# Planes of h's second block in the triple buffers, an earlier combine, and four seven-product pairs in feed-forward groups 5 and 9

## Chip, cores and metric

The kernel runs on one core of one Trainium2 chip. The metric is the device time of one execution in microseconds. The time before is 2090.94 us, the median of three runs (2088.95 to 2092.37).

## What is computed

A trunk of two pre-norm residual layers on x of 1 x 256 x 2048 in float32, and a final RMS norm. Layer 0 mixes with sliding-window attention beside an mLSTM, layer 1 with forgetting attention (FoX). The change lies in what follows each mixer: the output projection and the SwiGLU feed-forward network (FFN, hidden width 5632).

```python
for layer in range(2):
    xn = rms_norm(h, norm_mix[layer])
    mix = swa_mlstm(xn) @ w_out_even  if layer == 0 else  fox(xn) @ w_out_odd
    h = h + mix
    xn = rms_norm(h, norm_ffn[layer])
    h = h + (silu(xn @ w_gate[layer]) * (xn @ w_up[layer])) @ w_down[layer]
return rms_norm(h, norm_final)
```

## The kernel before

**Precision.** Each float32 operand is split into two fp32r parts, hi = cast(x) and lo = x - hi; a product takes three matmuls, hi·xh, lo·xh and hi·xl, of 128 x 128 weights of the moving side against 512 columns. Weights stream from memory: `load_raw` (L145) issues a DMA of 512 KB (two k-tiles by 512 columns) on SyncE's queue (SP), ScalarE (ACT) casts hi (L206), VectorE (DVE) subtracts to get lo (L207), and TensorE (PE) reads both. A split chunk lives in one of five slots of the stock.

**FFN groups.** The 5632 hidden columns are 11 groups of 512, in parts of 3, 4 and 4 (groups 0 to 2, 3 to 6, 7 to 10); behind each part stand two down-projection groups of the same build. `pair_group` works one group as eight pairs of k-tiles, each pair against two weight matrices (gate and up). A *plain* pair takes two chunks and 24 matmuls. A *seven-product* pair (kind 1, a Strassen-like scheme) takes 21 matmuls: both chunks are loaded into one raw buffer of the list `quads` (`quad`, 128 x 2048), three quarters of it are cast and subtracted as one 128 x 1536 operation into a triple buffer (L380 on ACT, L381 on DVE; the triples are `hi0`, `lo0` and `hi1`, `lo1`, used in turn), then DVE forms differences in place in the raw buffer (L645 on 128 x 1024, L648 and L649 on 128 x 512), and two 128 x 1024 casts and subtractions (L380, L381 again) fill two slots. Its seven products go into the group's four accumulators `plain` and into four further ones, `prods`. Sums of x that the scheme needs are made once per layer (`sx`, and `x4` for pair 7).

`ORDER` sets the pairs of a group: seven-product pairs stand at places 1, 3 and 5 of 0 to 7. `HEAVY` has them at places 0, 2, 4 and 6; a group in `DENSE` uses it, and `DENSE` is empty. `combine` (L575 to L592) merges `prods` into a tile c: ACT copies prods[0] (L577), DVE adds prods[3] (L579), prods[2] (L580) and prods[1] (L581). In a gate/up or down group (`halves` is None) it is called behind the loop over the pairs. DVE then adds the four `plain` accumulators to c (L696), and silu and the product with up follow (L698, L700). The eight banks of the accumulators change roles from group to group: the banks of `prods` hold `plain` of the next group and the other way round.

**Output projection and start of the FFN.** `out_proj` makes h in four blocks n = 0 to 3 of 512 columns. For each, `split_turned` copies the 16-bit planes of the block into a scratch `box` (L338, ACT), turns them with four DMA transposes of 128 x 4 x 128 (L340, SP's queue), and a `join` put off by `LATER` steps puts the planes together again (L345, ACT) and splits them into xh and xl (ACT L386, DVE L387). `scrap` (L365 to L376) gives the box: n = 0 and 2 use c, n = 3 uses `sd0` and `sd1`, which nothing else needs by then, and n = 1 a buffer with the tag `quad`, one of the two that `quads` gets later. A third raw buffer, `own`, is taken from a place of the weight pool (`wp`, tag `hi`); `quads` is in turn Q0, own, Q1.

**What sets the order.** Code order sets priorities; the framework's scheduler then orders each engine's instructions by its own estimate of when each can run, and PE, DVE, ACT and SP each work through their list in order. Buffers force waits: a load into a `quad` buffer that served as a box comes behind the join that reads it.

Of the kernel before, what the change touches and what calls it, by code (L numbers as in the profile page):

```python
# [7 lines left out]
F32 = mybir.dt.float32  # L8
BF16 = mybir.dt.bfloat16
F32R = mybir.dt.float32r  # L10
# [7 lines left out]
P = 128  # L18
# [5 lines left out]
NB = 512  # L24
CK = 2
# [10 lines left out]
ORDER = ((0, 0), (1, 1), (0, 2), (1, 3), (0, 4), (1, 5), (0, 6), (0, 7))  # L36
HEAVY = ((1, 1), (0, 0), (1, 3), (0, 2), (1, 5), (0, 4), (1, 7), (0, 6))
FOURTH = 7
DENSE = ()
DOWN = {  # L40
    6: ((0, 0), (1, 1), (0, 2), (1, 3), (0, 4), (0, 5)),
    8: ((0, 0), (1, 1), (0, 2), (1, 3), (0, 4), (1, 5), (0, 6), (0, 7)),
# [12 lines left out]
QUADS = 2  # L55
# [13 lines left out]
def mixed_of(order):  # L69
    return [p for w, p in order if w]  # L70
# [5 lines left out]
def trunk(  # L76
# [27 lines left out]
    stock, triples, quads = [], [], []  # L104
# [94 lines left out]
    def load_chunk(w, k0, c0, n):  # L199
        raw = ahead.pop(0) if ahead else load_raw(w, k0, c0, n)  # L200
        return raw if isinstance(raw, tuple) else split_chunk(raw, n)
# [10 lines left out]
    def two_banks(par, name):  # L212
        return [(pm if par else pa).tile([P, NB], F32, tag="pm" if par else "acc", name=name) for _ in range(2)]
# [153 lines left out]
    def scrap(fp, n):  # L367
        if n % 2 == 0:
            box = fp.tile([P, 4, NB], F32, tag="c", name="box", bufs=1)
            halves = box[:, 0:2, :], box[:, 2:4, :]  # L370
        elif n == 3:
            halves = [fp.tile([P, 3, NB], F32, tag=f"sd{i}", name="box", bufs=1)[:, 0:CK, :] for i in range(2)]
        else:
            box = fp.tile([P, 2 * CK, NB], F32, tag="quad", name="box", bufs=QUADS)
            halves = box[:, 0:2, :], box[:, 2:4, :]
        flat, turned = (a.rearrange("p a n -> p (a n)") for a in halves)  # L376
        return flat, turned.bitcast(U16).rearrange("p (b k t q) -> p b k t q", b=2, t=NT, q=P)

# [177 lines left out]
    def three(o, ah, al, hi, lo, start, stop):  # L556
        nc.tensor.matmul(o, ah, hi, start=start, stop=False)  # L557
        nc.tensor.matmul(o, ah, lo, start=False, stop=False)  # L558
        nc.tensor.matmul(o, al, hi, start=False, stop=stop)  # L559

    def pair_group(fp, par, lhs, sums, mats, order, todo=(), halves=None, inner=None, raws=None):
# [3 lines left out]
        def fresh(*at):  # L565
            known = at in begun
            begun.add(at)
            return not known

        todo = list(todo)  # L570
        prods = None
        kinds = [kind for kind, _ in order]
# [20 lines left out]

        for pos, (kind, pair) in enumerate(order):
            k0 = 2 * pair
            if inner is not None and pos == len(order) - 1:
                c = combine(prods)
                inner()
            if not kind:
# [4 lines left out]
                for m, (w, c0) in enumerate(mats):  # L604
                    hi, lo = load_chunk(w, k0, c0, NB)
# [10 lines left out]
            if first:  # L616
                if 1 - par and halves:
                    prods = [pm.tile([P, NB], F32, tag="pm", name="prod") for _ in range(4)]
                else:
                    prods = two_banks(1 - par, "prod") + two_banks(1 - par, "prod")  # L620
# [40 lines left out]
            three(prods[2], sh[2], sl[2], *parts[3], first, last)  # L661
            three(prods[3], sh[1], sl[1], *parts[2], first, last)
            three(plain[0][1], xa[:, t1], la[:, t1], *parts[0], fresh(0, 1), False)
        if inner is None:
            c = combine(prods)
        return plain, c

    def ffn(layer, fp, sx, x4, sd, key, todo, idx_next=None, key_next=None, finish=None):
# [8 lines left out]
        for g0, g1 in zip(PARTS, PARTS[1:]):  # L677
# [3 lines left out]
            for g in range(g0, g1):  # L681
                par = (g1 - 1 - g) % 2
                plain, c = pair_group(
                    fp,
                    par,
                    x_of,
                    sums_x,
                    [(w_gate[layer], g * NB), (w_up[layer], g * NB)],
                    HEAVY if g in DENSE else ORDER,
                    todo,  # L690
# [105 lines left out]
    def close_layer(layer, w_out, idx, key, **rest):  # L796
        with tc.tile_pool(name=f"fp{layer}", bufs=2) as fp:
            junk_of[:] = fp, "tmp", 2
            nx = len(mixed_of(ORDER))
            nd = max(len(mixed_of(o)) for o in DOWN.values())  # L800
            sx = [fp.tile([P, nx, 4, P], F32R, name=f"sx{i}", bufs=1) for i in range(2)]
            x4 = fp.tile([P, 2, P], F32R, name="x4", bufs=1)
            todo = out_proj(w_out, idx, key, (*sx, x4, fp))
            sd = [fp.tile([P, nd, 4, P], F32R, tag=f"sd{i}", name=f"sd{i}", bufs=1) for i in range(2)]
            triples.extend([fp.tile([P, 3, NB], F32R, name=f"{a}{i}", bufs=1) for a in ("hi", "lo")] for i in range(2))
            stock.extend([slot() for _ in range(5)])
            own = wp.tile([P, 2, CK, NB], F32R, tag="hi", name="raw").rearrange("p a k n -> p (a k) n").bitcast(F32)
            quads.extend(fp.tile([P, 2 * CK, NB], F32, tag="quad", name="raw", bufs=QUADS) for _ in range(QUADS))
            quads.insert(1, own)
            ffn(layer, fp, sx, x4, sd, key, todo, **rest)  # L810
            stock.clear()
            triples.clear()
            quads.clear()
# [3 lines left out]
    hi, lo = slot()  # L817
# [17 lines left out]
    with tc.tile_pool(name="ev", bufs=1) as ev:  # L835
# [225 lines left out]
        with tc.tile_pool(name="mp", bufs=1) as mp:  # L1061
# [8 lines left out]
            halves = spare_halves()  # L1070
# [11 lines left out]
            c = pair_even(OFF_QM, OFF_KM, MIXQ, [(G3_AT, gates_3)])  # L1082
# [30 lines left out]
            c = pair_even(OFF_OM, OFF_VM, MIXV, todo)  # L1113
# [80 lines left out]
    with tc.tile_pool(name="od", bufs=1) as od:  # L1194
# [70 lines left out]
        halves = spare_halves()  # L1265
# [9 lines left out]
        for i in range(4):  # L1275
            qt = od.tile([P, 4, S], F32, tag="qt", name="qtf")
            kt = od.tile([P, 4, S], F32, tag="kt", name="ktf")
            c = pair_nat(i * NB, FOX_H * FD + i * NB, todo if i == 0 else [(P_JOIN, join_p)] if join_p else (), MIX if i else MIX0, rest)
# [12 lines left out]
            if i == 0:  # L1291
                todo, later[:] = list(later), []
                c = pair_nat(c_v, c_v + NB, todo)
# [124 lines left out]
```

## Time and profile before

| | |
|---|---|
| time before, median of 3 runs | 2090.94 us (2088.95 to 2092.37) |
| time of the profiled execution | 2090.14 us |
| its span, first to last instruction | 2088.4 us |
| granted TensorE clock, mean | 0.998 |
| busy: PE / DVE / ACT | 2071.4 / 1806.3 / 1367.1 us |
| read from memory | 408.68 MB, 197 GB/s |

Times within the span are counted in microseconds from its first instruction. "Idle before" is the engine's wait ahead of an instruction, and the name behind the arrow is what ended it. In a table by stretches, each engine has its busy time and in brackets the number of instructions; "PEclk" is the clock that was granted to TensorE. The busy time of a matmul of 128 x 512 shows as 389 ns although they start some 0.226 us apart (184 in 41.50 us), since they overlap.

### The profile page before, as it was taken

The numbers are of one execution on the slowest core, as the hardware profiler recorded it, in microseconds if no ns is written. First come the engines' busy times: TensorE is split into PE (matmuls) and PEld (weight loads), VectorE is DVE, ScalarE is ACT, GpSimd is POOL, SyncE is SP. The second block draws the span as 40 slices with busy tenths as digits, with TensorE's granted clock in tenths as the row PEclk, the third lists the DMA queues.
The fourth block names the chain that finished last, engine by engine and source line by source line (L and its number), as shares of the span: only waits on it lengthen the run. The fifth ranks groups of instructions, "written<-read, shape, count | busy, mean of one in ns | idle before, by whom it ended". The sixth has DMA issues, their size and how long they took to land.

```text
span 2088.4 us, 26470 instructions
## 1 busy us (share of the span) xinstructions
PE 2071.4 (99%) x9473; PEld 1714.7 (82%) x9473; DVE 1806.3 (86%) x2169; ACT 1367.1 (65%) x1649; POOL 44.0 (2%) x69
## 2 busy tenths in 40 slices
PE   9999999999999999999999999999999999999998
PEld 7878887888888888888888888877888888888887
DVE  6788768989999989998899688679989999999984
ACT  6777677665577646667677676587655667556763
POOL 1010000000000000000000001000000000000000
PEclk9999999999999999999999999999999999999999
DMA  8566577765677666665676776585756766666754
GB/s 292 174 207 194 188 242 215 222 200 198 205 221 224 210 194 224 217 209 184 203 202 218 225 200 185 155 269 188 250 188 196 233 196 217 226 205 200 235 158 159
DMA packets 309572, 434.84 MB, mean 208 GB/s; under 512 B 106413, under 2 KB 114625, under 8 KB 309313
## 3 DMA queue, kind: packets, MB, share of 16 engines
q1 hardware_dynamic: 307088, 426.27, 65.1%
q0 software_dynamic: 1632, 5.80, 0.9%
q8 instruction: 74, 1.21, 0.2%
q10 hardware_dynamic: 720, 1.09, 0.2%
q14 instruction: 58, 0.47, 0.1%
HBM read 408.68 MB, written 2.12 MB: 197 GB/s over the span
## 4 chain that ended last, share of the span: by engine, by line
PE 89%; ACT 4%; DVE 3%; DMA 2%; issue 2%; SPq 0%; POOL 0%; POOLq 0%; ACTq 0%; DVEq 0%
PE acc L558 20%; PE acc L559 20%; PE acc L557 20%; PE prod L558 5%; PE prod L557 5%; PE prod L559 5%; PE acc L245 4%; PE acc L244 4%; PE acc L246 4%; DVE hi L207 1%; ACT box L345 1%; PE p L411 1%; ACT hi L206 1%; ACT hi L380 1%; DMA raw<-in_w_gate_dram 1%
## 5 line engine op out<-in xcount | busy, mean ns | idle before, releaser
L206 ACT CAST hi<-raw 128x1024 fp32r<-128x1024 f32 (+3 forms) x561 | 567.1, 1023 | 366.5 <-PE acc L559 179.4
L207 DVE TENSOR_TENSOR hi<-raw,hi 128x1024 fp32r<-128x1024 f32 (+3 forms) x561 | 657.9, 1186 | 137.2 <-ACT hi L206 134.7
L559 PE MATMUL acc<-hi,xl 128*128 128x512 f32 x1320 | 511.9, 389 | 0.0
L557 PE MATMUL acc<-hi,xh 128*128 128x512 f32 x1320 | 495.9, 390 | 0.8 <-ACT xh L386 0.6
L380 ACT CAST hi<-raw 128x1024 fp32r<-128x1024 f32 (+2 forms) x299 | 344.9, 1168 | 225.8 <-PE acc L559 192.7
L558 PE MATMUL acc<-hi,xh 128*128 128x512 f32 x1254 | 488.0, 390 | 0.2 <-DVE hi L207 0.2
L557 PEld LDWEIGHTS acc<-hi,xh 128*128 128x128 f32 x1320 | 247.6, 188 | 53.5 <-ACT xh L386 1.8
L559 PEld LDWEIGHTS acc<-hi,xl 128*128 128x128 f32 x1320 | 248.0, 188 | 51.5
L558 PEld LDWEIGHTS acc<-hi,xh 128*128 128x128 f32 x1254 | 235.4, 188 | 50.0 <-DVE hi L207 1.0
L381 DVE TENSOR_TENSOR hi<-raw,hi 128x1024 fp32r<-128x1024 f32 (+1 forms) x204 | 240.2, 1180 | 11.1 <-ACT hi L380 10.4
L381 DVE TENSOR_TENSOR lo<-raw,hi 128x1536 fp32r<-128x1536 f32 x95 | 166.6, 1754 | 43.6 <-ACT hi L380 40.0
L559 PE MATMUL acc<-hi,ml 128*128 128x512 f32 x466 | 181.0, 389 | 0.0
L557 PE MATMUL acc<-hi,mh 128*128 128x512 f32 x466 | 173.3, 389 | 0.0
L558 PE MATMUL acc<-hi,mh 128*128 128x512 f32 x437 | 170.3, 390 | 0.4 <-DVE hi L207 0.4
L245 PE MATMUL acc<-hi,mh 128*128 128x512 f32 (+1 forms) x322 | 126.3, 392 | 0.0
L244 PE MATMUL acc<-hi,mh 128*128 128x512 f32 (+1 forms) x322 | 125.8, 391 | 0.0
L246 PE MATMUL acc<-hi,ml 128*128 128x512 f32 (+1 forms) x322 | 123.7, 391 | 0.0
L645 DVE TENSOR_TENSOR raw<-raw 128x1024 f32<-128x1024 f32 x95 | 115.5, 1217 | 0.4
L557 PEld LDWEIGHTS acc<-hi,mh 128*128 128x128 f32 x466 | 87.5, 188 | 18.6 <-ACT hi L206 0.4
L559 PEld LDWEIGHTS acc<-hi,ml 128*128 128x128 f32 x466 | 87.5, 188 | 18.1
L245 PE MATMUL acc<-hi,xh 128*128 128x512 f32 (+3 forms) x288 | 99.8, 347 | 0.2 <-DVE hi L207 0.2
L246 PE MATMUL acc<-hi,xl 128*128 128x512 f32 (+3 forms) x288 | 99.1, 345 | 0.0
(364 smaller groups left out, 3073.9 us busy)
## 6 DMA issues: line engine op xcount, KB each, us to landing
raw<-in_w_gate_dram SPq DMA_DIRECT2D x176, 512.0 KB, 4.3
raw<-in_w_up_dram SPq DMA_DIRECT2D x176, 512.0 KB, 4.8
raw<-in_w_down_dram SPq DMA_DIRECT2D x176, 512.0 KB, 4.8
raw<-in_w_in_odd_dram SPq DMA_DIRECT2D x88, 512.0 KB, 5.2
raw<-in_w_in_even_dram SPq DMA_DIRECT2D x51, 512.0 KB, 5.0
raw<-in_w_out_even_dram SPq DMA_DIRECT2D x32, 512.0 KB, 5.3
raw<-in_w_out_odd_dram SPq DMA_DIRECT2D x32, 512.0 KB, 4.7
hr<-in_w_in_even_dram SPq DMA_DIRECT2D x12, 512.0 KB, 4.4
```

The costliest lines, as they stand in the source:

```text
L206: latest[0] = nc.scalar.copy(hi[:, k, 0:n], raw[:, k, 0:n])
L207: nc.vector.tensor_tensor(out=lo[:, k, 0:n], in0=raw[:, k, 0:n], in1=hi[:, k, 0:n].bitcast(F32), op=ALU.subtract)
L244: nc.tensor.matmul(o, ah[:, ts], hi, start=(k == 0), stop=False)
L245: nc.tensor.matmul(o, ah[:, ts], lo, start=False, stop=False)
L246: nc.tensor.matmul(o, al[:, ts], hi, start=False, stop=(k == k_all - 1 and cs.stop == n))
L345: nc.scalar.copy(ju[:, :, b], turned[:, b, :, :, :].rearrange("p k t q -> p (k t q)"))
L380: cast = nc.scalar.copy(dst_h, src)
L381: nc.vector.tensor_tensor(out=dst_l, in0=src, in1=dst_h.bitcast(F32), op=ALU.subtract)
L557: nc.tensor.matmul(o, ah, hi, start=start, stop=False)
L558: nc.tensor.matmul(o, ah, lo, start=False, stop=False)
L559: nc.tensor.matmul(o, al, hi, start=False, stop=stop)
L645: nc.vector.tensor_tensor(out=raw[:, 1:4:2, :], in0=raw[:, 3:4, :].broadcast_to([P, 2, NB]), in1=raw[:, 1:3, :], op=ALU.subtract)
```

## The change

Four edits. `DENSE` becomes (5, 9), so that groups 5 and 9 of both layers take pair 7 as a fourth seven-product pair. The box of h's second block (n = 1) is taken from the second triple (`hi1` for the planes, `lo1` for the turned ones) and no longer from a `quad` buffer; the triples get tags for that. `combine` of a gate/up or down group is called right behind the last seven-product pair: ahead of place 6 of `ORDER`, of place 7 of `HEAVY`, of place 4 of the six-pair down groups. And `own` becomes the third of the raw buffers: Q0, Q1, own.

```diff
--- before.py
+++ after.py
@@ -36,7 +36,7 @@
 ORDER = ((0, 0), (1, 1), (0, 2), (1, 3), (0, 4), (1, 5), (0, 6), (0, 7))
 HEAVY = ((1, 1), (0, 0), (1, 3), (0, 2), (1, 5), (0, 4), (1, 7), (0, 6))
 FOURTH = 7
-DENSE = ()
+DENSE = (5, 9)
 DOWN = {
     6: ((0, 0), (1, 1), (0, 2), (1, 3), (0, 4), (0, 5)),
     8: ((0, 0), (1, 1), (0, 2), (1, 3), (0, 4), (1, 5), (0, 6), (0, 7)),
@@ -371,8 +371,7 @@
         elif n == 3:
             halves = [fp.tile([P, 3, NB], F32, tag=f"sd{i}", name="box", bufs=1)[:, 0:CK, :] for i in range(2)]
         else:
-            box = fp.tile([P, 2 * CK, NB], F32, tag="quad", name="box", bufs=QUADS)
-            halves = box[:, 0:2, :], box[:, 2:4, :]
+            halves = [fp.tile([P, 3, NB], F32, tag=f"{a}1", name="box", bufs=1)[:, 0:CK, :] for a in ("hi", "lo")]
         flat, turned = (a.rearrange("p a n -> p (a n)") for a in halves)
         return flat, turned.bitcast(U16).rearrange("p (b k t q) -> p b k t q", b=2, t=NT, q=P)
 
@@ -593,6 +592,8 @@
 
         for pos, (kind, pair) in enumerate(order):
             k0 = 2 * pair
+            if 1 not in kinds[pos:] and 1 in kinds[pos - 1 : pos] and halves is None:
+                c = combine(prods)
             if inner is not None and pos == len(order) - 1:
                 c = combine(prods)
                 inner()
@@ -661,7 +662,7 @@
             three(prods[2], sh[2], sl[2], *parts[3], first, last)
             three(prods[3], sh[1], sl[1], *parts[2], first, last)
             three(plain[0][1], xa[:, t1], la[:, t1], *parts[0], fresh(0, 1), False)
-        if inner is None:
+        if inner is None and halves is not None:
             c = combine(prods)
         return plain, c
 
@@ -802,11 +803,11 @@
             x4 = fp.tile([P, 2, P], F32R, name="x4", bufs=1)
             todo = out_proj(w_out, idx, key, (*sx, x4, fp))
             sd = [fp.tile([P, nd, 4, P], F32R, tag=f"sd{i}", name=f"sd{i}", bufs=1) for i in range(2)]
-            triples.extend([fp.tile([P, 3, NB], F32R, name=f"{a}{i}", bufs=1) for a in ("hi", "lo")] for i in range(2))
+            triples.extend([fp.tile([P, 3, NB], F32R, tag=f"{a}{i}", name=f"{a}{i}", bufs=1) for a in ("hi", "lo")] for i in range(2))
             stock.extend([slot() for _ in range(5)])
             own = wp.tile([P, 2, CK, NB], F32R, tag="hi", name="raw").rearrange("p a k n -> p (a k) n").bitcast(F32)
             quads.extend(fp.tile([P, 2 * CK, NB], F32, tag="quad", name="raw", bufs=QUADS) for _ in range(QUADS))
-            quads.insert(1, own)
+            quads.append(own)
             ffn(layer, fp, sx, x4, sd, key, todo, **rest)
             stock.clear()
             triples.clear()
```

Counted over the program, PE has 12 matmuls of 128 x 512 fewer (three for each of four groups); DVE has 16 instructions more and ACT four, those of four seven-product pairs in place of plain ones; SP's count of 973 stays. Lines behind L592 stand one further, and L377 to L592 one less: L380 and L381 of before are L379 and L380 after, L577 is L576.

Three places show how the order moves. The first is SP's queue in layer 0, at the end of the output projection's first half; the eight transposes are four for each block. `box_2579` and `box_2647` are the boxes of n = 0 and 1, `raw_2993` of before is Q0, `raw_2994` and `raw_2995` of after are Q0 and Q1. Before:

```order
L145 DMA raw_2764<-in_w_out_even_dram 128x2x512
L145 DMA raw_2781<-in_w_out_even_dram 128x2x512
L340 DMA_TRANSPOSE box_2579<-box_2579 128x4x128 x4
L340 DMA_TRANSPOSE box_2647<-box_2647 128x4x128 x4
L145 DMA raw_2798<-in_w_out_even_dram 128x2x512
L145 DMA raw_2815<-in_w_out_even_dram 128x2x512
L145 DMA raw_2832<-in_w_out_even_dram 128x2x512
L145 DMA raw_2869<-in_w_out_even_dram 128x2x512
L145 DMA raw_2993<-in_w_gate_dram 128x2x512
L145 DMA raw_2993<-in_w_up_dram 128x2x512
L145 DMA raw_2886<-in_w_out_even_dram 128x2x512
```

After:

```order
L145 DMA raw_2697<-in_w_out_even_dram 128x2x512
L145 DMA raw_2994<-in_w_gate_dram 128x2x512
L145 DMA raw_2714<-in_w_out_even_dram 128x2x512
L145 DMA raw_2994<-in_w_up_dram 128x2x512
L145 DMA raw_2731<-in_w_out_even_dram 128x2x512
L145 DMA raw_2995<-in_w_gate_dram 128x2x512
L145 DMA raw_2995<-in_w_up_dram 128x2x512
L145 DMA raw_2748<-in_w_out_even_dram 128x2x512
L145 DMA raw_2765<-in_w_out_even_dram 128x2x512
L340 DMA_TRANSPOSE box_2579<-box_2579 128x4x128 x4
L340 DMA_TRANSPOSE box_2648<-box_2647 128x4x128 x4
L145 DMA raw_2782<-in_w_out_even_dram 128x2x512
```

Both loads of the first two seven-product pairs (four DMAs) now stand ahead of the eight transposes, and one more load of w_out stands behind them.

The second is ACT some 30 us later, where the joins of n = 2 (`box_2922`, after: `box_2923`) and of n = 3 (`box_2969`/`box_2970`, after: `box_2970`/`box_2971`) stand among the casts for group 0. Before, where `raw_2992` is `own`, of the second seven-product pair, and `raw_2994` is Q1, of the third:

```order
L206 CAST hi_2987<-raw_3088 128x1024
L380 CAST hi0_2983<-raw_2994 128x1536
L345 COPY box_2969<-box_2970 128x1024 x2
L206 CAST hi_2990<-raw_3156 128x1024
L380 CAST hi1_2985<-raw_2992 128x1536
L345 COPY box_2922<-box_2922 128x1024 x2
L386 ACTIVATE xh_58<-box_2969,gT_93 128x256 x4
L206 CAST hi_2991<-raw_3172 128x1024
L386 ACTIVATE xh_58<-box_2922,gT_93 128x256 x4
```

After, where `raw_2995` is Q1, of the second pair, and `raw_2993` is `own`, of the third:

```order
L206 CAST hi_2988<-raw_3089 128x1024
L345 COPY box_2923<-box_2923 128x1024 x2
L379 CAST hi_2989<-raw_2995 128x1024
L385 ACTIVATE xh_58<-box_2923,gT_93 128x256 x4
L326 ACTIVATE full_3119<-box_2923,gT_93 128x256 x2
L379 CAST hi_2990<-raw_2995 128x1024
L206 CAST hi_2991<-raw_3157 128x1024
L379 CAST hi0_2984<-raw_2993 128x1536
L345 COPY box_2970<-box_2971 128x1024 x2
L206 CAST hi_2992<-raw_3173 128x1024
L379 CAST sx0_2332<-s4_3122 128x512
L385 ACTIVATE xh_58<-box_2970,gT_93 128x256 x4
```

The 128 x 1536 cast of the second pair has gone from this place (it stands 15 rows further up, a few rows behind the join of n = 1, whose box it overwrites), the join of n = 2 has come ahead of that of n = 3, and the second pair's 128 x 1024 casts stand ahead of the latter.

The third is DVE at the beginning of group 5 in layer 0, right behind the drain of group 4's last accumulator into c. Before:

```order
L696 TENSOR_TENSOR c_4905<-acc_4633,c_4905 128x512
L207 TENSOR_TENSOR hi_2991<-raw_5014,hi_2991 128x1024
L700 SCALAR_TENSOR_TENSOR c_4905<-c_4905,r_2998 128x512
L381 TENSOR_TENSOR lo1_2986<-raw_2993,hi1_2985 128x1536
L700 SCALAR_TENSOR_TENSOR c_4905<-c_4905,r_2998 128x512
L381 TENSOR_TENSOR hi_2987<-raw_2994,hi_2987 128x1024
L645 TENSOR_TENSOR raw_2993<-raw_2993 128x2x512
L648 TENSOR_TENSOR raw_2993<-raw_2993 128x512
L381 TENSOR_TENSOR hi_2988<-raw_2994,hi_2988 128x1024
L649 TENSOR_TENSOR raw_2993<-raw_2993 128x512
L207 TENSOR_TENSOR hi_2989<-raw_5062,hi_2989 128x1024
L207 TENSOR_TENSOR hi_2990<-raw_5078,hi_2990 128x1024
```

After:

```order
L697 TENSOR_TENSOR c_4831<-acc_4634,c_4831 128x512
L380 TENSOR_TENSOR lo1_2987<-raw_2994,hi1_2986 128x1536
L701 SCALAR_TENSOR_TENSOR c_4831<-c_4831,r_2999 128x512
L207 TENSOR_TENSOR hi_2989<-raw_5047,hi_2989 128x1024
L646 TENSOR_TENSOR raw_2994<-raw_2994 128x2x512
L701 SCALAR_TENSOR_TENSOR c_4831<-c_4831,r_2999 128x512
L380 TENSOR_TENSOR lo0_2985<-raw_2995,hi0_2984 128x1536
L649 TENSOR_TENSOR raw_2994<-raw_2994 128x512
L380 TENSOR_TENSOR hi_2992<-raw_2993,hi_2992 128x1024
L380 TENSOR_TENSOR hi_2990<-raw_2994,hi_2990 128x1024
L646 TENSOR_TENSOR raw_2995<-raw_2995 128x2x512
L207 TENSOR_TENSOR hi_2988<-raw_5031,hi_2988 128x1024
```

Before, one subtraction of 128 x 1536 and two plain chunks (L207) stand here behind the drain, besides a third ahead of it; after, two of the former and two of the latter, so the raw work of two seven-product pairs (L646, L649) has moved close together.

## The prediction

> **What bounds the kernel now.** I read the page first, for the engine that sets the end.
>
> ```profile
> span 2088.4 us, 26470 instructions
> ...
> PE 2071.4 (99%) x9473; PEld 1714.7 (82%) x9473; DVE 1806.3 (86%) x2169; ACT 1367.1 (65%) x1649; POOL 44.0 (2%) x69
> ...
> L558 PE MATMUL acc<-hi,xh 128*128 128x512 f32 x1254 | 488.0, 390 | 0.2 <-DVE hi L207 0.2
> ```
>
> PE is busy 99% of the span, and over 1254 matmuls with a lo operand it waited 0.2 us for DVE. So only two things are worth anything: fewer matmuls, and the few places where PE stands still. DVE at 86% is close behind, so work that is given to it needs cover. I then read the stretches around the start of the FFN in layer 0 (330 to 362 us) and layer 1 (1400 to 1424), beside the present groups 5 (602.0) and 9 (850.9).
>
> ```profile
> 330.00:340.00 10.00, 9.14 (x41) 7.24 (x39) 6.14 (x8) 6.01 (x6) 0.69 (x1) 1.00 0.82 220
> 340.00:350.00 10.00, 7.36 (x23) 4.86 (x24) 9.82 (x17) 10.00 (x16) 0.00 (x0) 0.83 0.54 178
> 350.00:362.00 12.00, 11.01 (x49) 8.69 (x48) 12.00 (x14) 9.20 (x12) 0.00 (x0) 1.00 0.51 177
> ```
>
> ```profile
> 1400.00:1412.00 12.00, 10.52 (x44) 7.46 (x43) 11.41 (x19) 12.00 (x19) 0.00 (x0) 1.00 0.53 176
> 1412.00:1424.00 12.00, 11.47 (x47) 8.21 (x46) 12.00 (x16) 9.85 (x12) 0.00 (x0) 1.00 0.53 177
> ```
>
> ```profile
> 602.00:643.50 41.50, 41.50 (x184) 34.36 (x184) 40.43 (x45) 28.51 (x28) 0.00 (x0) 1.00 0.73 226
> 850.90:892.40 41.50, 41.50 (x184) 34.36 (x183) 39.25 (x44) 28.16 (x28) 0.00 (x0) 1.00 0.68 216
> ```
>
> In a steady group PE is busy all the time: 41.50 us / 184 = **0.2255 us per matmul**. At that rate the 32 us from 330 would hold 142 matmuls; 41 + 23 + 49 = 113 ran, 29 short: **6.5 us lost** in layer 0. In layer 1, 24 us hold 106.4, 91 ran: 15.4 short, **3.5 us lost**. The single waits come from PE's rows in time.
>
> ```profile
> 341.17 0.50 PE L557 MATMUL prod<-hi,xh 128*128 128x512 f32 x1 [2.03 <-ACT hi L380]
> ...
> 342.96 0.80 PE L558 MATMUL prod<-lo,xh 128*128 128x512 f32 x1 [0.83 <-DVE lo L381]
> 343.56 0.63 PE L559 MATMUL prod<-hi,xl 128*128 128x512 f32 x1
> 343.98 0.63 PE L558 MATMUL acc<-lo,xh 128*128 128x512 f32 x1
> ...
> 346.53 0.50 PE L557 MATMUL acc<-hi,xh 128*128 128x512 f32 x1 [0.64 <-ACT xh L386]
> ...
> 355.40 0.50 PE L558 MATMUL prod<-hi,sx 128*128 128x512 f32 x1 [0.99 <-DVE hi L381]
> ```
>
> The first two waits are for the cast and the subtraction of the second seven-product pair, the third for xh of h's third block (n = 2), the fourth for a late slot. Together 4.5 us; behind them matmuls start 0.42 us apart for a while, at a granted clock of 0.83 in that stretch. The Trainium skill ("TensorE: Matmul & The Clock Gate", Part 1) says that the clock halves after an idle window of about 3.4 us and returns after a busy one. The trace agrees in kind (0.42 us against 0.2255), though here gaps of 2.03 and 0.83 us were enough; by that rule the slow matmuls vanish with the gaps, which the count of 29 already contains.
>
> Why the pair is late stands in the rows of SP's queue and of ACT.
>
> ```profile
> 280.48 10.37 SPq L340 DMA_TRANSPOSE box<-box  x8
> 290.94 2.06 SPq L145 DMA_DIRECT2D raw<-in_w_out_even_dram  x4
> ...
> 323.47 5.61 SPq L340 DMA_TRANSPOSE box<-box  x4
> 329.18 0.53 SPq L145 DMA_DIRECT2D raw<-in_w_gate_dram  x1
> 329.80 5.14 SPq L340 DMA_TRANSPOSE box<-box  x4
> 335.00 0.58 SPq L145 DMA_DIRECT2D raw<-in_w_up_dram  x1
> ```
>
> ```profile
> 336.28 2.56 ACT L345 COPY box<-box 128x1024 uint16<-128x1024 uint16 x2 [3.99 <-DMA box<-box]
> 338.70 1.04 ACT L206 CAST hi<-raw 128x1024 fp32r<-128x1024 f32 x1
> 339.64 1.47 ACT L380 CAST hi<-raw 128x1536 fp32r<-128x1536 f32 x1
> 341.01 2.55 ACT L345 COPY box<-box 128x1024 uint16<-128x1024 uint16 x2
> 343.43 1.70 ACT L386 ACTIVATE xh<-box,gT 128x256 fp32r<-128x256 f32 x4
> ```
>
> The pair's raw buffer is `own`; its up load is issued at 335.00, behind the four transposes of n = 3, and its cast runs at 339.64, just ahead of the wait that ends at 341.17. ACT meanwhile takes the join of n = 3 first (idle 3.99 us for it) and that of n = 2 only at 341.01, though the latter's transposes were issued six us earlier. In layer 1 ACT shows the same:
>
> ```profile
> 1397.71 1.48 ACT L380 CAST hi<-raw 128x1536 fp32r<-128x1536 f32 x1 [2.31 <-DMA raw<-in_w_up_dram]
> 1399.10 5.01 ACT L345 COPY box<-box 128x1024 uint16<-128x1024 uint16 x4
> ```
>
> **The change, part by part.** *Box and `own`.* The order of the changed kernel issues the loads of the first two pairs ahead of the first transposes, some 55 us before 335.00, casts the second pair behind the join of n = 1 instead of at 339.64, and joins n = 2 ahead of n = 3. `own` is now the third pair, whose loads still stand behind both blocks of transposes. So its cast falls at about 339 to 340.5, but PE reads it two pairs later, and a pair is 21 to 24 matmuls, 4.7 to 5.4 us. The waits for the second pair go wholly, that for xh of n = 2 (its join some ten us earlier) too. Next late is the third pair: with the stalls gone PE comes to it earlier, and by my walk through the new order it is ready 0.4 to 3 us ahead. I take 6.0 of the 6.5 us in layer 0 and, where that margin is thinner, 3.0 of 3.5 in layer 1. Bounds: all of it, or what rival one leaves.
>
> What moves for that: one load of w_out goes from ahead of the eight transposes to behind them, that is from 279 to about 291 us. The first load now behind them was ready for ACT at:
>
> ```profile
> 296.27 1.05 ACT L206 CAST hi<-raw 128x1024 fp32r<-128x1024 f32 x1 [1.89 <-DMA raw<-in_w_out_even_dram]
> ```
>
> Cast 1.05 us and subtraction 1.22 make it 298.6; PE wants the chunk that now stands there at about 299.1 (12 matmuls, 2.7 us, earlier than the one that stood there). Cover 0.5 us here, 1.6 in layer 1 by the same walk. I charge **0.3 us**.
>
> *Four pairs in groups 5 and 9.* Each saves three matmuls: 4 x 3 x 0.2255 = **2.7 us** on PE. Each costs DVE this:
>
> ```profile
> L207 DVE TENSOR_TENSOR hi<-raw,hi 128x1024 fp32r<-128x1024 f32 x525 | 633.4, 1219 | 127.5 <-ACT hi L206 125.2 <-DMA hv<-room 0.4
> L381 DVE TENSOR_TENSOR hi<-raw,hi 128x1024 fp32r<-128x1024 f32 x190 | 230.6, 1217 | 11.1 <-ACT hi L380 10.4
> L381 DVE TENSOR_TENSOR lo<-raw,hi 128x1536 fp32r<-128x1536 f32 x95 | 166.6, 1754 | 43.6 <-ACT hi L380 40.0 <-DMA raw<-in_w_down_dram 2.0 <-DMA raw<-in_w_gate_dram 1.2
> L645 DVE TENSOR_TENSOR raw<-raw 128x1024 f32<-128x1024 f32 x95 | 115.5, 1217 | 0.4
> L649 DVE TENSOR_TENSOR raw<-raw 128x512 f32<-128x512 f32 x95 | 64.8, 682 | 0.1
> ```
>
> 1.75 + 1.22 + 2 x 0.68 (L648 has L649's shape) + 2 x 1.22 = 6.77 us in place of two subtractions of L207, 2.44: **+4.3 us of DVE**. Group 5 then holds 40.4 + 4.3 = 44.7 us of DVE work for 41.5 - 0.7 = 40.8 us of PE, group 9 43.6: short by 3.9 and 2.8 us. The cover is DVE's lead over PE.
>
> ```profile
> L206 ACT CAST hi<-raw 128x1024 fp32r<-128x1024 f32 x525 | 545.4, 1050 | 348.7 <-PE acc L559 174.9 <-PE acc L246 44.4 <-issue 41.7
> ```
>
> ACT's longest waits are for PE to free slots, so the stock runs full: a lead between one chunk (12 matmuls, 2.7 us) and four (10.8 us). With one chunk the four groups stall 2 x 1.2 + 2 x 0.1 = 2.6 us, with four none; I take the middle of the lower half and charge **1.0 us**. The groups behind have 1.1 to 2.3 us of DVE idle time each in which the lead comes back. ACT's extra cast of 1.5 us hides in its 13 idle us of a group.
>
> *Early combine.* It moves the same four instructions of a group ahead of one or two plain pairs. Banks of `prods` become free earlier, but nothing waited for them (the 0.2 us above), and in the trace ACT's copy already runs in mid-group. Worth nothing alone; in 5 and 9, whose next prods come at place 0 of the group, it keeps c and the drain from being late there.
>
> **Sum**, against the profiled execution's own 2090.14 us (span 2088.4; 0.8 below the median of the runs, inside their scatter of 3.4): -6.0 - 3.0 - 2.7 + 1.0 + 0.3 = -10.4, so **2079.7 us**.
>
> **Rivals.** *One: the stalls only move.* From 340 to 362 DVE is busy 9.82 of 10 and 12.00 of 12 us, ACT 10.00 of 10: once the second pair is early, their backlog is late instead, and gains are only the idle time that can be filled beforehand, DVE's 3.9 us of 330 to 340 in layer 0 and half of layer 1's loss, 1.75. Against it: the cast, subtraction and differences of the second pair (some 6 us of each side) leave that very stretch. Time: 2090.1 - 3.9 - 1.8 - 2.7 + 1.3 = 2083.0.
>
> *Two: the dense groups become DVE's.* If the lead is gone when they begin, 2 x (3.9 + 2.8) = 13.4 us replace the 1.0: 2090.1 - 9.0 - 2.7 + 13.4 + 0.3 = 2092.1; with half of that lead 2085.4. For it speaks DVE's 1.1 us of idle time in group 5; against it the 0.2 us that PE ever waited for L207.
>
> *Three: the output projection pays; this ends slower.* ACT now casts the first pair ahead of the planes of n = 0. If its load lands late, all of ACT behind it waits, then the transposes, then all loads of w_out behind these on SP.
>
> ```profile
> 271.86 1.05 ACT L206 CAST hi<-raw 128x1024 fp32r<-128x1024 f32 x1 [1.01 <-PE acc L246]
> 276.84 2.01 ACT L206 CAST hi<-raw 128x1024 fp32r<-128x1024 f32 x2 [3.93 <-PE acc L246]
> ```
>
> ACT has 3.93 us of room there; beyond it each us of delay d costs PE one, less the covers of 0.5 and 1.6. To end over 4.2 us above the old time it must eat 10.7 us of gain and 4.2 more: 2d = 14.9 + 2.1, d = 8.5 us per layer. At d = 9 the time is 2090.1 - 10.7 + 15.9 = 2095.3. The Trainium skill ("TensorE: Matmul & The Clock Gate", table at the head, engine queue depth) calls ScalarE's queue strict FIFO, which is this rival's condition, and the 3.99 us of idle time at 336.28 agree. Against it: the loads are issued from about 267 us, over 5 us ahead.
>
> *Four: the box edit doesn't do what it says,* as the second pair still comes late in the run for another of its buffers: -2.7 + 1.0 and a third of the starts' 9.0, 2085.4.
>
> **How the numbers follow.** Forecast 0.62; rival one 0.13; two 0.10, of which 0.04 on the faster side; three 0.09, of which 0.08 slower; four 0.06, faster or same by halves. A measurement of this kernel tells about 0.2%, 4.2 us, from no change. Faster: 0.62 + 0.13 + 0.04 + 0.03 = 0.82; same: 0.06 + 0.01 + 0.03 = 0.10; slower 0.08. The range goes from 2075.0, all 10.0 us of the starts, 2.7 and some of the other small waits (2.4), to 2088.5, which takes in rivals one, four and half of two.
>
> **What would show it.** Right: windows of 330 to 362 and 1400 to 1424 with full counts of matmuls, the second pair's cast near 310 us, n = 2 joined before n = 3, groups 5 and 9 at 40.8 us each. Wrong: PE waiting for L207 or L381 within groups 5, 6, 9 or 10; ACT idle before the first 128 x 1536 cast for more than 4 us; PE idle between 295 and 310 us behind the moved load of w_out.

## The result and the profile after

The changed kernel takes 2087.94 us, the median of 20 runs, against 2091.82 for the kernel before on the same chip: ratio 0.9982, 95% interval 0.9975 to 0.9988, 3.9 us faster where the forecast's sum was 10.4. One of the 20 runs took 5138.99 us, in a slow state, and is left out of the ratio. The time lies just inside the stated range, but at its upper end, which had been set to take in the rivals. The profiled execution took 2088.39 us (before: 2090.14, which is 1.7 below the median of 2091.82, so the two traces differ by 1.7 us only). The head of the page after:

```profile
span 2086.7 us, 26379 instructions
...
PE 2068.0 (99%) x9461; PEld 1713.3 (82%) x9461; DVE 1820.1 (87%) x2185; ACT 1370.7 (66%) x1653; POOL 44.3 (2%) x69
```

PE's busy time fell by 3.4 us, the span by half of that: something new stands still. First the stretches on which the forecast rested, the two starts and layer 0's groups 5 and 6 after the change:

```profile
330.00:340.00 10.00, 10.00 (x46) 8.29 (x45) 5.64 (x12) 9.84 (x15) 0.69 (x1) 1.00 0.60 137
340.00:350.00 10.00, 10.00 (x46) 8.29 (x45) 7.74 (x10) 8.00 (x13) 0.00 (x0) 1.00 1.05 392
350.00:362.00 12.00, 12.00 (x55) 9.93 (x54) 12.00 (x18) 10.57 (x12) 0.00 (x0) 1.00 0.52 171
```

```profile
1400.00:1412.00 12.00, 12.00 (x55) 9.94 (x54) 11.47 (x17) 11.77 (x20) 0.00 (x0) 1.00 0.93 317
1412.00:1424.00 12.00, 11.19 (x47) 8.30 (x46) 12.00 (x18) 10.28 (x13) 0.00 (x0) 1.00 0.43 127
```

```profile
598.20:639.00 40.80, 40.80 (x182) 33.78 (x181) 39.57 (x45) 29.16 (x29) 0.00 (x0) 1.00 0.65 216
639.00:681.30 42.30, 41.82 (x185) 34.30 (x184) 40.66 (x43) 28.52 (x29) 0.00 (x0) 1.00 0.69 224
```

Layer 0's start is whole: 147 matmuls in 32 us where 113 ran. (These sums over neighbouring stretches count a matmul on a border twice; 330 to 362 as one stretch holds 143, and held 111.) Layer 1's got 102 where 91 ran, and still loses some. The dense group 5 takes exactly the forecast 40.8 us with no wait, but group 6 behind it loses 0.8. PE's three longest waits between 200 and 1040 us, summed by line, are now these:

```profile
PE acc L556 <- ACT mh L379: 3.4, 1, 3.4
PE acc L244 <- DVE h L394: 2.0, 1, 2.0
PE acc L556 <- ACT hi L206: 0.5, 1, 0.5
```

None of the three was there before. Measured from start to start of neighbouring matmuls, with those that start 0.43 us apart behind a wait included, the account of the two traces is: start of layer 0 -7.2 us, of layer 1 -1.5 (4.1 to 2.6), 12 matmuls -2.7; a new loss near 281 us +3.9, one near 963 us +4.2, and 0.75 in each layer's group 6, +1.5. The sum is -1.8, against -1.7 between the spans.

**The loss near 281 us** is in the output projection of layer 0. Before, DVE's first additions of h's blocks waited for nothing but PE:

```profile
276.62 1.29 DVE L395 TENSOR_TENSOR h<-acc,h 128x512 f32<-128x512 f32 x2 [2.45 <-PE acc L246]
```

After the change, SP, ACT, DVE and PE in order of time:

```profile
268.93 0.46 SPq L145 DMA_DIRECT2D raw<-in_w_up_dram  x1
```

```profile
276.27 1.48 ACT L379 CAST hi<-raw 128x1536 fp32r<-128x1536 f32 x1 [3.87 <-DMA raw<-in_w_up_dram]
```

```profile
277.78 1.76 DVE L380 TENSOR_TENSOR lo<-raw,hi 128x1536 fp32r<-128x1536 f32 x1 [4.12 <-ACT hi L379]
279.57 1.22 DVE L646 TENSOR_TENSOR raw<-raw 128x1024 f32<-128x1024 f32 x1
280.72 1.28 DVE L394 TENSOR_TENSOR h<-acc,h 128x512 f32<-128x512 f32 x2
```

```profile
281.46 0.50 PE L244 MATMUL acc<-hi,mh 128*128 128x512 f32 x1 [1.99 <-DVE h L394]
...
283.51 0.63 PE L245 MATMUL acc<-hi,mh 128*128 128x512 f32 x1
283.93 0.63 PE L246 MATMUL acc<-hi,ml 128*128 128x512 f32 x1
```

The up load of the first seven-product pair is issued at 268.93 and has landed at 276.27, 7.3 us later. The cast waits for it, the subtraction for the cast, and behind the subtraction on DVE stand the additions (L394) that take block 0 of h out of its banks. PE needs these banks for the second half of the projection and waits 1.99 us; then matmuls start 0.43 us apart until 286, since the granted clock is 0.50 from 282.77 to 286.18 (0.83 on average from 280 to 290).

**The loss near 963 us** is in the first down group of layer 0's last part. Its last two pairs need the transposed hidden block of group 10: the drain of the accumulators, the products, the transposes, the joining copies (L736) and the cast to `mh` form a chain. Before, DVE's drain of group 10 and the products behind it, and ACT's cast of the joined block:

```profile
935.51 1.87 DVE L696 TENSOR_TENSOR c<-acc,c 128x512 f32<-128x512 f32 x3
...
939.58 1.59 DVE L700 SCALAR_TENSOR_TENSOR c<-c,r 128x512 f32<-128x512 f32 x2
```

```profile
953.39 1.06 ACT L380 CAST mh<-c 128x1024 fp32r<-128x1024 f32 x1
```

After, the same steps on DVE, SP and ACT, and PE's wait:

```profile
938.83 1.88 DVE L697 TENSOR_TENSOR c<-acc,c 128x512 f32<-128x512 f32 x3
940.62 1.75 DVE L380 TENSOR_TENSOR lo<-raw,hi 128x1536 fp32r<-128x1536 f32 x1
942.29 0.75 DVE L701 SCALAR_TENSOR_TENSOR c<-c,r 128x512 f32<-128x512 f32 x1
...
946.36 0.75 DVE L701 SCALAR_TENSOR_TENSOR c<-c,r 128x512 f32<-128x512 f32 x1
```

```profile
948.87 1.50 SPq L145 DMA_DIRECT2D raw<-in_w_down_dram  x3
950.59 5.99 SPq L732 DMA_TRANSPOSE turned<-c  x4
```

```profile
949.52 1.99 ACT L730 COPY c<-c 128x1024 uint16<-128x1024 uint16 x2
...
957.82 2.56 ACT L737 COPY c<-turned 128x1024 uint16<-128x1024 uint16 x2 [2.14 <-DMA turned<-c]
...
962.54 1.05 ACT L379 CAST mh<-c 128x1024 fp32r<-128x1024 f32 x1
```

```profile
963.65 0.50 PE L556 MATMUL acc<-hi,mh 128*128 128x512 f32 x1 [3.44 <-ACT mh L379]
```

The drain ends at 940.7 where it ended at 937.4, although PE, by the order of its matmuls, was 4.4 us further by then. The last product ends at 947.1, where it was 941.2. From drain to cast the chain takes 21.8 us instead of 16.0. So against PE the cast is 9.2 + 4.4 = 13.6 us later; before, it ended 10.0 us ahead of the matmul that needs it, so it is now 3.6 late.

Two things make the chain longer. On DVE other pairs' work has slid in between the two products (2.6 us). And from the first transpose's issue to the cast it takes 12.0 us instead of 9.1: before, the transposes landed 2.4 to 2.5 us after their issue; now three loads of 512 KB are issued right ahead of them (948.87), the last lands at 956.6, and the transposes behind them take 6.6 to 3.9 us. Layer 1 of the same run shows what this is worth. Its drain is nearly as late against PE (20.4 us ahead of the need, where layer 0 has 19.3 and both had 27.1 before), but no load is issued in the six us ahead of its transposes:

```profile
2012.98 5.12 SPq L732 DMA_TRANSPOSE turned<-c  x4
```

They land in 2.4 to 2.5 us, the cast runs at 2021.36, 8.4 us behind the first, and ends 1.4 us before PE needs it. With 8.4 us instead of 12.0 layer 0's cast would, by estimate, have been just in time. So DVE's delay eats the room in both layers, and the transposes behind the loads turn it into a wait in one.

### The profile page after: what moved, and what is told of

The parts are those of the page before. It is cut to its first block, busy times and chain, and to the rows that moved or that the text cites. A ratio compares the mean times of both kernels' runs of the same rounds, so it can differ in the third digit from the quotient of the medians.

```text
span 2086.7 us, 26379 instructions
## 1 busy us (share of the span) xinstructions
PE 2068.0 (99%) x9461; PEld 1713.3 (82%) x9461; DVE 1820.1 (87%) x2185; ACT 1370.7 (66%) x1653; POOL 44.3 (2%) x69
## 4 chain that ended last, share of the span: by engine, by line
PE 88%; DVE 4%; DMA 3%; ACT 3%; issue 2%; SPq 0%; POOL 0%; POOLq 0%; ACTq 0%; DVEq 0%
PE acc L557 20%; PE acc L558 20%; PE acc L556 20%; PE prod L556 5%; PE prod L557 5%; PE prod L558 5%; PE acc L244 4%; PE acc L245 4%; PE acc L246 4%; DVE hi L207 1%; DMA raw<-in_w_up_dram 1%; PE p L410 1%; ACT hi L206 1%; DMA raw<-in_w_gate_dram 0%; DVE lo L380 0%
## 5 line engine op out<-in xcount | busy, mean ns | idle before, releaser
L206 ACT CAST hi<-raw 128x1024 fp32r<-128x1024 f32 (+3 forms) x553 | 559.6, 1023 | 349.1 <-PE acc L558 201.1
L207 DVE TENSOR_TENSOR hi<-raw,hi 128x1024 fp32r<-128x1024 f32 (+3 forms) x553 | 651.3, 1187 | 128.7 <-ACT hi L206 126.4
L379 ACT CAST hi<-raw 128x1024 fp32r<-128x1024 f32 (+2 forms) x311 | 359.4, 1169 | 224.0 <-PE acc L558 125.2
L558 PE MATMUL acc<-hi,xl 128*128 128x512 f32 x1296 | 502.5, 389 | 0.0
L556 PE MATMUL acc<-hi,xh 128*128 128x512 f32 x1296 | 479.4, 390 | 1.2 <-ACT hi L206 1.2
L557 PE MATMUL acc<-hi,xh 128*128 128x512 f32 x1226 | 477.4, 390 | 1.3 <-DVE hi L207 1.3
L556 PEld LDWEIGHTS acc<-hi,xh 128*128 128x128 f32 x1296 | 243.0, 188 | 52.6 <-ACT hi L206 2.5
L558 PEld LDWEIGHTS acc<-hi,xl 128*128 128x128 f32 x1296 | 243.3, 188 | 50.4
L557 PEld LDWEIGHTS acc<-hi,xh 128*128 128x128 f32 x1226 | 230.2, 188 | 50.3 <-DVE hi L207 2.6
L380 DVE TENSOR_TENSOR hi<-raw,hi 128x1024 fp32r<-128x1024 f32 (+1 forms) x212 | 250.2, 1184 | 16.6 <-ACT hi L379 16.1
L380 DVE TENSOR_TENSOR lo<-raw,hi 128x1536 fp32r<-128x1536 f32 x99 | 173.6, 1754 | 35.2 <-ACT hi L379 35.0
L646 DVE TENSOR_TENSOR raw<-raw 128x1024 f32<-128x1024 f32 x99 | 120.5, 1219 | 0.2
```

The lines of the kernel that those rows point to most:

```text
L206: latest[0] = nc.scalar.copy(hi[:, k, 0:n], raw[:, k, 0:n])
L207: nc.vector.tensor_tensor(out=lo[:, k, 0:n], in0=raw[:, k, 0:n], in1=hi[:, k, 0:n].bitcast(F32), op=ALU.subtract)
L379: cast = nc.scalar.copy(dst_h, src)
L380: nc.vector.tensor_tensor(out=dst_l, in0=src, in1=dst_h.bitcast(F32), op=ALU.subtract)
L646: nc.vector.tensor_tensor(out=raw[:, 1:4:2, :], in0=raw[:, 3:4, :].broadcast_to([P, 2, NB]), in1=raw[:, 1:3, :], op=ALU.subtract)
```

## The experiments

All times are medians, with the ratio of each to the kernel before on the same chip.

| run | what differs | us | ratio (95%) |
|---|---|---|---|
| before | | 2091 to 2092 | 1 |
| the change | | 2087.94 | 0.9982 (0.9975 to 0.9988) |
| e1 | the change, `DENSE = ()` | 2084.34 | 0.9967 (0.9954 to 0.9979) |
| e2 | box and own alone | 2085.30 | 0.9970 (0.9959 to 0.9982) |
| e3 | `DENSE` alone | 2094.73 | 1.0018 (1.0009 to 1.0027) |
| e4 | `DENSE` and early combine | 2095.25 | 1.0019 (1.0010 to 1.0028) |
| e5 | e1, box in hi0 and lo1 | 2081.61 | 0.9954 (0.9941 to 0.9966) |
| e6 | the change, `DENSE = (5, 8)` | 2084.32 | 0.9968 (0.9955 to 0.9980) |
| e7 | own alone | 2085.88 | 0.9974 (0.9965 to 0.9984) |
| e8 | box alone | 2090.64 | 0.9998 (0.9989 to 1.0006) |
| e9 | own and early combine | 2084.07 | 0.9963 (0.9949 to 0.9977) |
| e10 | e5 with `DENSE = (4, 8)` | 2083.75 | 0.9961 (0.9948 to 0.9974) |
| e11 | the change, `DENSE = (9,)` | 2086.34 | 0.9976 (0.9967 to 0.9985) |
| e12 | the change, box in hi0 and lo1 | 2085.44 | 0.9971 (0.9959 to 0.9982) |

My theory after the result: two independent losses, one from the fourth pairs' work on DVE (near 963 us and in groups 6), one from the first pair's early load (near 281 us). The rival for the first was the early combine, which also moved what stands around the drain.

**e1, the change without dense groups.**

```diff
-DENSE = (5, 9)
+DENSE = ()
```

> The changed kernel with DENSE = () again, all else kept. Theory: the 3.4 us wait of PE near 963 us (cast of mh, last part of layer 0) and the two waits of 0.65 us in groups 6 come from the fourth pairs' work on DVE, which makes the drain and the turn of group 10 late. Then they go (-4.2 and -1.6 us), the 12 matmuls come back (+2.7), and the wait of 2 us near 281 us stays: about 2084.8 us against 2087.9 for the change. Rival, that the early combine's new order makes group 10's turn late: the wait near 963 us stays, and the time is about 2089.0.

2084.34 us, 3.6 faster than the change itself. The same block's cast in e1, and the two stretches of PE's new losses, in both of which e1 ran at the full clock:

```profile
949.53 1.04 ACT L379 CAST mh<-c 128x1024 fp32r<-128x1024 f32 x1
```

```profile
270.00:290.00 20.00, 18.32 (x81) 14.82 (x80) 13.16 (x15) 12.59 (x15) 0.00 (x0) 1.00 0.67 217
...
955.00:965.00 10.00, 10.00 (x46) 8.29 (x45) 9.82 (x10) 5.72 (x6) 0.00 (x0) 1.00 0.81 272
```

The cast is 13 us earlier than after the change, with the early combine still in place, and PE has no wait around 963; the one near 281 is there. The theory holds and the rival falls. (In e1's trace the transposes of this block have no load close ahead and land in 2.4 to 2.5 us again.)

**e2, box and own without combine and dense groups.**

```diff
 quads.insert(1, own)  ->  quads.append(own)
 box of n = 1: tag "quad"  ->  tags "hi1", "lo1"
```

> The kernel before with the box of n = 1 in the second triple and own last, with neither the early combine nor the fourth pairs. Theory: the early combine is worth nothing, so this is e1 within 1 us, 2084.8, with the wait near 281 us and without that near 963. Rival, early combine to blame for the wait near 963 us: 2084.8 here, but e1 at 2089.

2085.30, 1.0 us from e1 and with overlapping intervals: here the early combine is worth about a microsecond or nothing.

**e3 and e4, the dense groups on the kernel before,** without and with the early combine.

```diff
-DENSE = ()
+DENSE = (5, 9)
```

> The kernel before with DENSE = (5, 9) alone. Theory: waits at the start of both feed-forward networks stay as before (7.2 and 4.1 us), no wait near 281 us, a wait of about 4 us at the last part of layer 0 and small ones in group 6, 2.7 us of matmuls saved: 2091.8 - 2.7 + 1.6 + 4.2 = 2094.9 us. Rival, that the fourth pairs are harmless by themselves: 2089.1 us.

> The kernel before with DENSE = (5, 9) and the early combine, box and own as before. Theory: as e3 within 1 us if the early combine is worth nothing in the dense groups either, 2094.9. Rival, that it relieves the banks of the dense groups: several us faster than e3, near 2090.

2094.73 and 2095.25: both slower than before, by amounts that the theory gave to a few tenths. PE's longest wait in e3, between 200 and 1040 us:

```profile
PE acc L557 <- ACT mh L380: 2.9, 1, 2.9
```

The wait for mh is there without box, own and combine; the next one, 1.7 us for L380, is the old one of the start. That the combine's place does anything for the dense groups doesn't show. In all five runs with a wait for mh near 963 us (the change, e3, e4, e11, e12) three loads are issued in the 3 us ahead of the transposes, and the first of these takes 5.2 to 6.6 us to land; in the nine others at most one load is, and it takes 2.4 to 3.0. No run moved the loads alone.

**e5, another box.** The planes of n = 1 in `hi0`, the turned ones in `lo1`, on e1. The loads stay early, but the first pair's cast cannot precede the join of n = 1, and on DVE its subtraction moves behind the additions.

```diff
-for a in ("hi", "lo")]   with tag=f"{a}1"
+for a in ("hi0", "lo1")] with tag=a
```

> e1 with the box of n = 1 in hi0 and lo1 in place of hi1 and lo1. The loads of the first two pairs stay as early as in the change, but the cast of the first pair now has to wait for the join of n = 1, and in the new order its subtraction and differences stand behind the four additions of h's first two blocks on DVE. Theory: the wait of PE near 281 us is DVE standing in line behind a subtraction whose data are late, so it goes, and about 2.2 us with it: 2082.3. Rival, that the early transfers themselves delay the weights of the output projection: the wait stays near 281 us, 2084.3 or later.

2081.61, the fastest of all, with the additions and the stretches as follows:

```profile
276.34 1.29 DVE L394 TENSOR_TENSOR h<-acc,h 128x512 f32<-128x512 f32 x2 [2.45 <-PE acc L246]
```

```profile
270.00:290.00 20.00, 20.00 (x90) 16.55 (x89) 11.20 (x12) 14.16 (x18) 0.00 (x0) 1.00 0.87 281
330.00:362.00 32.00, 31.69 (x140) 25.61 (x138) 28.42 (x41) 27.21 (x37) 0.69 (x1) 1.00 0.80 254
```

The additions wait for PE itself again, at 276.34 instead of 280.72, and PE loses nothing near 281, though the DMA engines carry more there (281 GB/s; 217 in e1) and the first pair's up load lands at 275.8, as late as after the change (276.2). It was the place in DVE's line, not the traffic.

**e6 and e11, which dense group costs what.**

```diff
-DENSE = (5, 9)
+DENSE = (5, 8)     (e6)
+DENSE = (9,)       (e11)
```

> The change with DENSE = (5, 8): the same number of fourth pairs, but an ordinary group 9 between the second dense group and the last group of the part. Theory: DVE's extra work is caught up in group 9, the turn of group 10 is in time and the 4.2 us near 963 us go; groups 6 keep their 0.65 us each and group 9 may get such: 2083.7 to 2085. Rival, that the backlog does not shrink in one group or that group 10's turn is late for another reason: 2087.9.

> The change with DENSE = (9,). Theory: the wait near 963 us belongs to group 9 alone and the 0.65 us in groups 6 to group 5: e1 - 1.35 + 4.2 = about 2087.2, with no wait in groups 6. Rival, that the wait near 963 us needs both dense groups: 2083.

e6 takes 2084.32, as expected, and has no wait for mh; the dense groups then cost what they save (e1: 2084.34). PE waits for chunks instead, 1.1 us for ACT's casts (L206), one of them in group 6, the other of 0.6 at 998 us. e11 takes 2086.34, 0.9 below the figure expected, with this as the longest wait between 200 and 1040 us:

```profile
PE acc L556 <- ACT mh L379: 2.0, 1, 2.0
```

Group 9 alone is enough for the wait for mh, though it is 2.0 us here and 3.4 with both; no wait is left in group 6, so that one was group 5's.

**e7, e8 and e9: which edit mends the starts.** own alone, box alone, and own with the early combine.

```diff
 quads.append(own)                            (e7, e9)
 box of n = 1 in "hi1", "lo1"                 (e8)
 combine behind the last seven-product pair   (e9)
```

> The kernel before with quads in the order Q0, Q1, own, nothing else. Theory: the late second pair was an affair of the order of buffers alone; its load goes ahead of the transposes of n = 2 and 3, the starts lose only about 1 and 2.5 us, and no early load means no wait near 281 us: about 2083. Rival, that Q1 is needed free of the box as well: the starts keep most of their 7.2 and 4.1 us, 2090 or more.

> The kernel before with the box of n = 1 in the second triple, nothing else; own stays second. Theory: the second pair still loads among the last transposes, so the starts keep most of their waits, and the wait near 281 us is added: 2091.4 + 2.2 = about 2093.6. Rival, that the box is what frees the start: near 2085.

> e7 (own last, box in a quad buffer) with the early combine added. e7 shows new waits of PE at the ends of groups 0 and 2 and at the joins behind, for DVE's first addition of combine (410, 468 and 471 us, the like in layer 1), some 4.6 us in all. Theory: they come from combine standing late behind the pairs, so the early one takes them away: 2085.9 - 4 = about 2082. Rival, that they come from DVE's backlog and not from combine's place: 2085 to 2086.

own alone takes 2085.88, 3 us more than expected: the start of layer 0 holds 136 matmuls instead of 111, nearly what the theory asked, but new waits come at groups 0 and 2. The box alone takes 2090.64, net nothing: it gives 125 there but brings the wait near 281 us:

```profile
270.00:290.00 20.00, 17.84 (x72) 14.31 (x71) 13.18 (x15) 11.88 (x16) 0.00 (x0) 0.91 0.70 229
330.00:362.00 32.00, 29.99 (x125) 22.62 (x124) 25.58 (x36) 27.93 (x36) 0.69 (x1) 1.00 0.62 175
```

That was 3 us less than I expected for e8, since the box alone mends a part of layer 0's start. e9 takes 2084.07, where the theory said 2082: of e7's new waits

```profile
PE acc L557 <- ACT mh L380: 0.8, 1, 0.8
PE acc L557 <- DVE c L579: 0.5, 1, 0.5
```

the one for combine's addition went in layer 0 (in layer 1 it is 0.4) and the one for mh stayed at 0.7. The early combine gave 1.8 us between medians whose intervals overlap; in the traces the stretch from 400 to 480 us holds 350 matmuls for 345, 1.1 us, and the like in layer 1 one more. How much of it is real stays open.

**e10 and e12: dense groups once the 281 us are mended.**

```diff
 box of n = 1 in "hi0", "lo1"
-DENSE = (5, 9)
+DENSE = (4, 8)     (e10; e12 keeps (5, 9))
```

> e5 (box in hi0 and lo1, early combine, own last) with fourth pairs in groups 4 and 8, each with an ordinary group between it and the last of its part. Theory: the extra 4.3 us of DVE are caught up in groups 5 and 9, the last groups' turns are in time, and of the 2.7 us of matmuls some 1 us is lost near 998 us as in e6: about 2080. Rival, that any dense group costs what it saves, as 5 and 8 did: 2081.6.

> The change with the box of n = 1 in hi0 and lo1, else as it is. Theory: the two losses have nothing to do with each other, so only that near 281 us goes: 2087.9 - 2.7 = about 2085.2, with the wait near 963 us as before. Rival, that they share a cause (a DVE that never catches up): both go, 2081 or less.

e12, 2085.44, is the change minus 2.5 us: the loss near 281 is gone, that for mh is there (2.4 us in its trace), so the two are independent. e10, 2083.75, misses the theory by 3.8 us and lies 2.1 above its rival too: no wait for mh, but from 560 us on PE's longest waits are

```profile
PE acc L557 <- DVE hi L207: 2.0, 4, 0.8
```

for chunks. Against e5 two dense groups per layer cost 2.1 us net instead of saving 2.7. e10's lowest run, 2082.03, lies above e5's highest, 2082.01, but the intervals (0.9948 to 0.9974 and 0.9941 to 0.9966) overlap: a saving of the full 2.7 us would hardly fit them, and that the groups cost something is not shown.

## Why the prediction was wrong

**Box and own, layer 0: right.** -6.0 of 6.5 was forecast, and 7.2 us went, for the reason given (the count of 29 matmuls short was low, since 142 was set against a sum that counts matmuls on borders twice; 147 less 113 is 34): the second pair was cast at 311 instead of 340 us, and n = 2 joined before n = 3. The two edits were not told apart, though, and most of the gain is `own`'s (e7: -5.1 us; e8: 0, some 3 us gained at the start and 4 lost near 281). Whether part of the mending is bought by PE's stop near 281 us stays open: that loss is 3.9 us in the change, with nothing lost at the start; but e1 and e11 lose 2.0 and 1.8 near 281, and 1.8 and 0.6 at the start, and e5, which has no stop, 0.8.

**Layer 1: half.** -3.0 was forecast, -1.5 came. I had named the thinner margin; DVE is busy 12.00 of 12 us from 1412 on and PE waits 1.0 us for L207, which is rival one's mechanism in this layer. The box edit has a share: counted from start to start, 1.1 us are left there with own alone (e7), 2.6 in the change.

**"I charge 0.3 us" for what moves: the first failed step.** The sum looked at the w_out load that moved behind the transposes and at ACT's 3.93 us of room, and ACT's cast at 276.27 shows that the room was nearly enough. It didn't ask what stands behind the pair's subtraction on DVE: the additions that free PE's banks, which ran at 276.62 before and at 280.72 after. The measured price is 3.9 us in the trace, of which 1.7 is the slow clock, and 2.7 between e1 and e5, where e1's trace shows 2.0 us lost near 281 at the full clock. This was rival three's condition (the load lands late) with another engine in the middle and a quarter of its price.

**"The cover is DVE's lead over PE ... I charge 1.0 us": the second failed step.** The 2.7 us of matmuls came: group 5 took 40.80 us, and the lead did cover the dense group. But the 4.3 us of extra work don't stop at the group's end; DVE gives them back during the next group, and there stands the chain from drain to silu, turn, join and cast, which has a due time. The sum looked for stalls inside the dense groups and put nothing down for this chain. DVE's delay took its 10 us of room, and with the transposes behind three loads that cost 4.2 us where group 9 precedes the last group of a part in layer 0; groups 6 cost 1.5: 5.7 instead of 1.0. "The groups behind have 1.1 to 2.3 us of DVE idle time each in which the lead comes back" held in count, but not in time. Between e1 and the change the dense groups cost 3.6 us net. Layer 1's last group made no wait; its transposes landed in 2.4 to 2.5 us: its cast ran 28 us behind the last matmul of group 10, layer 0's 33, and 3.6 of these 5 us lie between the transposes' issue and the cast. So part of the 4.2 us belongs to the loads ahead on SP's queue and not to DVE alone.

**Early combine, "worth nothing alone": right** within about 1 us in e1 against e2 and e3 against e4; in e9 against e7 perhaps 1.8.

**The sum against the traces.** -6.0 - 3.0 - 2.7 + 1.0 + 0.3 was forecast, -7.2 - 1.5 - 2.7 + 5.7 + 3.9 came. The gains were nearly right together, 11.4 for 11.7; the two small charges were the error, 9.6 us for 1.3. The range held because it was wide, and not because the sum did.

**Rivals.** One was true in part (layer 1, and the trade between 281 and 340 us). Two had the right payer and the wrong place. Four, that the box edit does not do what it says, fails in its reason: the second pair did come early, and the edit's gain was taken back near 281 us.

The fastest version, e5, keeps own last, the early combine and no dense group, and parks the box where it holds the first pair's subtraction back: 2081.61 us, 0.9954 of before.

## What to carry to other kernels

Work that is given to a nearly full engine can be paid for where the next due chain runs on it, not where it is added: follow the debt into the next stage, and through the queues that the chain passes, before counting a saving on another engine. A load that comes earlier brings its whole chain of instructions with it, and in queues worked in order each of them can stand in front of something that is due; look on every engine that the chain touches for who is queued behind it. And try edits singly: here one line (the order of the raw buffers) gave 5 us, one nothing net, and one took 3.6 back.

## What the runs showed of the hardware

The clock's answer to a wait was not a matter of the wait's length. After 1.99 us of waiting at 281.46 the changed kernel ran eight matmuls 0.43 us apart, at a granted clock of 0.50. The longer wait of 3.44 us at 963.65 left the clock whole, and so did e1's 1.7 us near 281 and e11's 1.98 at 960.59. So a wait of some 2 us cost 2.2 us near 281 in e6 and 3.9 in the change.

The clock records of the traces suggest what decides it. Ahead of the run's end, every stretch at 0.50 in the traces is 3.413 us long, or three times that (at the start of layer 0 in e3 and e4), and within a trace their starts lie whole multiples of 3.413 us apart: in the changed kernel the one at 282.77 and the one at the end of the run, 2081.59, are 527 such steps apart. So the clock seems to be set anew every 3.413 us. On this grid the wait of 1.99 us falls into one step, and the wait of 3.44 us is shared by two:

```profile
279.36:282.77 3.41, 1.42 (x7) 1.10 (x7) 3.38 (x6) 1.63 (x4) 0.00 (x0) 1.00 0.50 184
282.77:286.18 3.41, 3.41 (x10) 2.67 (x9) 3.41 (x5) 2.84 (x5) 0.00 (x0) 0.50 0.35 72
```

```profile
958.60:962.02 3.42, 1.60 (x8) 0.99 (x6) 0.71 (x1) 3.42 (x4) 0.00 (x0) 1.00 0.96 299
962.02:965.43 3.41, 1.78 (x8) 1.42 (x8) 3.41 (x4) 3.41 (x4) 0.00 (x0) 1.00 1.00 353
```

PE stood still for 2.0 us of the first step, and the next ran at 0.50; for 1.8 and 1.6 us of the other two, and nothing followed. Over all traces the clock fell after steps with 1.8 to 2.8 us without a matmul (the change, before, e3, e4, e8, e12) and stayed whole after those with 1.7 or less; at 1.8 both happened, and the ends of matmuls are modelled. That fits a limit near half a step, but no run was made to test it. Where the grid lies against a wait is then luck, and 1.7 of the 3.9 us near 281 were that.
